# Spreading a triangular solve over the projections' matmuls in the RWKV-7 layer of a two-layer decoder trunk

## Chip, cores and metric

The kernel runs on one core of one Trainium2 chip. The metric is the device time of one execution in microseconds (us); less is better.

## What is computed

The trunk has two layers on a sequence of 512 tokens and a model width of 2048. Each layer is `x + W_out(mixer(RMSNorm(x)) * silu(gate))`. The first layer's mixer is a differential attention, the second's is RWKV-7 time mixing with 32 heads of 64 channels. The change lies in the second layer alone. Its core is a recurrence on a 64x64 state `S` per head:

```python
def step(S, inp):
    r_t, w_t, k_t, v_t, a_t, b_t = inp
    sa = jnp.einsum('bhvk,bhk->bhv', S, a_t)
    S = S * w_t[:, :, None, :] + sa[..., None] * b_t[:, :, None, :] + v_t[..., None] * k_t[:, :, None, :]
    y = jnp.einsum('bhvk,bhk->bhv', S, r_t)
    return S, y
```

Around it, `p = h @ w_in` gives r, k, v and the gate (2048 columns each) and two small low-rank inputs; the token shift mixes each row with the one before; r, k, v and the decay enter the recurrence; the result is normalised per head, gated and projected with `w_out`. All of it is float32.

## The kernel before

**Precision and tiles.** A float32 product is made of three matmuls of split halves (`mm3`, line 129): every weight tile is cast by ScalarE (ACT) into a high half `wh` (line 115), and VectorE (DVE) subtracts it to get the low half `wl` (line 116). One projection of 128 columns takes 16 row blocks of 3 matmuls, so 48 matmuls of 128x512.

**Pairs.** The second layer (`layer1`) works on 16 pairs of heads, `j` = 0 to 15. For each pair it runs four projections on TensorE (PE): v, k of the next pair, the gate of pair `j - 3`, and r of the next pair. All else of the layer is put beside those 192 matmuls.

**Chunked recurrence.** The 512 steps are cut into 8 chunks of 64. For each pair:

- `gram` (line 1099) makes the products of keys and queries inside the chunks into `G`; ACT copies the parts that the solve needs into `LP` (line 1108).
- `t_solve` inverts the unit triangular matrices of all chunks at once, by halves of 32. On DVE it is one transposition into `LT` (line 1158), 31 dependent steps of two instructions each (line 1169 into `tmpl`, line 1171 into `Tm`), a scaling (line 1172) and two transpositions, into `T1` (line 1174; the profile calls the tile T) and `W` (line 1177). GpSimd (POOL) copies `W` into `TT` (line 1182).
- `t_first` (line 1196, PE tile `px`) and `t_second` (line 1211) join the halves; `t_first` reads `T1`, and `t_second` reads `W`.
- `scan_pair` is the recurrence over the chunks. Each chunk goes PE (line 1288), ACT (`rhs`, line 1291), PE (line 1299), ACT (`VS`, line 1301), PE (line 1306), DVE (two state updates into `VS`, one per head, line 1310; line 1313 for the first chunk). The next chunk's line 1288 reads both updates. POOL copies the state aside (`SA`, line 1294) and scales it (`Sg`, line 1297).

While pair `j` is solved, the scan of pair `j - 1` runs. A `Chain` holds the scan as a generator: it is advanced from `tick`, which `mm3` calls after each projection matmul, and each `yield` says how many matmuls are to pass before the next step (7 and 8 for most pairs).

**What sets the order.** The code is traced in Python; a scheduler then puts each engine's instructions in one queue by priority and by its own estimate of when each could start, and every engine works its queue strictly in that order. Priorities are offsets: `AHEAD` 2000 for the weight splits, `SCAN` 3000 for the steps of the scan, `SOLVE` 4000 for the whole of `t_solve`. `issue_after` and `add_manual_dep` with `NoSync` only bind the scheduler's order; no semaphore comes of them.

**Small work of a pair that matters below.** When the chunk's state update has been traced, one piece of `g.later` is traced behind it. The first piece, `decays`, is a DVE scan `l` (line 1049), `m` (1051) and a subtraction into `l` (1052), which ACT turns into `E` (lines 1053 and 1054), `l` (1055) and `BK` (1063). `norms` (lines 1019 and 1020) sums the squares of the keys, split by ACT into `sHx` (line 892) and by DVE into `sLx` (line 893).

Of the kernel before, what the change touches and what calls it, by code (L numbers as in the profile page):

```python
# [23 lines left out]
P = 128  # L24
# [11 lines left out]
    pass  # L36


AHEAD, SCAN, SOLVE = 2000, 3000, 4000


def ahead(offset):


    def deco(f):
        def g_(g, *a, **k):
            with g.tc.high_priority(offset=offset):
                return f(g, *a, **k)

        return g_  # L50

    return deco
# [34 lines left out]
class Halves:  # L87


    def __init__(self, parts, n):  # L90
        self.parts, self.n = parts, n
# [43 lines left out]
class Chain:  # L135
# [7 lines left out]
    def step(self, g):  # L143
        with g.tc.high_priority(offset=SCAN):
            self.wait = next(self.steps, None)
        if g.state and g.later:
            with g.tc.issue_after(g.state.ins):
                g.later.pop(0)()
        g.state = None
        if self.wait is None:  # L150
            g.chains.remove(self)

    def finish(self, g):
        while self.wait is not None:
            with g.tc.issue_after(g.m.ins):
                self.step(g)


def tick(g, m):

    g.m = m
    if g.chains:
        c = g.chains[0]
        c.wait -= 1
        if c.wait <= 0:
            with g.tc.issue_after(m.ins):
                c.step(g)
# [436 lines left out]
def flat(t):  # L604

    n = "abc"[: len(t.shape) - 1]
    n = " ".join(n)
    return t[:].rearrange(f"p {n} -> p ({n})").rearrange("p (k c) -> p k c", k=KG)
# [531 lines left out]
def turn_keys(g, p, c0):  # L1140

    nc = g.nc
    if not c0:
        p.BKT = g.work.tile([P, NC_, P], F32, name="BKT", tag="BKT", bufs=2)
    ps = g.ps.tile([P, 512], F32, name="pt", tag="pb", bufs=2)
    for i in range(4):
        nc.tensor.transpose(ps[:, i * P : (i + 1) * P], p.BK[:, c0 + i].rearrange("p s t -> p (s t)"), g.ident[:])
    nc.scalar.copy(p.BKT[:, c0 : c0 + 4], ps[:].rearrange("p (c k) -> p c k", c=4))


@ahead(SOLVE)
def t_solve(g, j, p):


    nc, w = g.nc, g.work
    NQ = HALF // NG
    LT = w.tile([P, HALF, HALF], F32, name="LT", tag="LT", bufs=1)
    nc.vector.transpose(LT[:].rearrange("p (r c) t -> p t r c", r=NG),  # L1158
                        p.LP[:].rearrange("p c t -> p t c")[:, :, None, :].to_broadcast([P, HALF, NG, NC_]))
    Tm = w.tile([P, NQ, HALF], F32, name="Tm", tag="Tm", bufs=1)  # L1160
    tmp = w.tile([P, NQ * HALF], F32, name="tmpl", tag="tmpl", bufs=1)
    nc.gpsimd.tensor_copy(Tm[:], g.unit[:])
    n2 = p.n2
    nc.vector.tensor_scalar(n2[:], n2[:], 1e-24, None, ALU.max)
    nc.vector.reciprocal(n2[:], n2[:])
    for i in range(HALF - 1):
        n, s = HALF - 1 - i, i // NG + 1
        tt = tmp[:, : n * s].rearrange("p (a b) -> p a b", a=s)
        nc.vector.scalar_tensor_tensor(tt, LT[:, i : i + 1, i + 1 :].to_broadcast([P, s, n]), n2[:, i : i + 1],  # L1169
                                       Tm[:, 0:s, i : i + 1].to_broadcast([P, s, n]), ALU.mult, ALU.mult)  # L1170
        nc.vector.tensor_add(Tm[:, 0:s, i + 1 :], Tm[:, 0:s, i + 1 :], tt)  # L1171
    nc.vector.tensor_mul(Tm[:], Tm[:], n2[:, None, :].to_broadcast([P, NQ, HALF]))
    p.T1 = w.tile([P, NC_, HALF], F32, name="T1", tag="T1", bufs=1)
    nc.vector.transpose(p.T1[:].rearrange("p c (q r) -> p q r c", r=NG),
                        Tm[:].rearrange("p q (r c) -> p q r c", r=NG))
    p.W = w.tile([P, NC_, HALF], F32, name="W", tag="Tm", bufs=1)
    nc.vector.transpose(p.W[:], p.T1[:])
    for h in range(2):
        for half in range(2):
            o = half * HALF  # L1180
            q = slice(h * C + o, h * C + o + HALF)
            nc.gpsimd.tensor_copy(g.TT[j % 2][q, :, h, o : o + HALF], p.W[q])
# [5 lines left out]
def t_first(g, j, p):  # L1188

    nc, w = g.nc, g.work  # L1190
    p.X = w.tile([P, NC_, HALF], F32, name="X", tag="X", bufs=1)
    p.px = px = g.ps.tile([P, 512], F32, name="px", tag="pd", bufs=1)
    N = NC_ * HALF
    for c in range(NC_):
        for h, b0, lo, hi in BLOCKS:
            nc.tensor.matmul(px[hi, c * HALF : (c + 1) * HALF], p.G[lo, c, 0, h, HALF:C], p.T1[lo, c, :],
                             start=True, stop=True, tile_position=(b0, b0 + HALF))
    for _, _, _, hi in BLOCKS:
        nc.scalar.copy(p.X[hi], px[hi, :N].rearrange("p (c s) -> p c s", c=NC_))
    for h, b0, _, _ in BLOCKS:  # L1200
        r_ = slice(b0, b0 + C)
        nc.scalar.copy(p.G[r_, :, 0, h, :], p.AR[r_, :, 0, :])
# [168 lines left out]
def layer1(g, aps):  # L1371
    nc, tc = g.nc, g.tc
    with ExitStack() as cx:
# [7 lines left out]
        def proj(i, j, **k):  # L1381
            return unit_chan(g, [(win, i * D + j * P, P)], P, **k)[0]
# [23 lines left out]
        for j in range(D // P):  # L1406
            p = pairs[j]
            if j:
                others = [(0, lambda p=p: turn_keys(g, p, 0)), (1, lambda p=p: turn_keys(g, p, 4)),
                          (4, lambda p=p: turn_values(g, p))]  # L1410
                if j > 1:
                    others.append((5, lambda i=j - 2: finish_y(g, i, pairs[i])))
                full = LAG <= j < D // P - 1
                gaps = (7, 8) if full else (5, 6) if j < LAG else (4, 5)
                chain(g, j - 1, pairs[j - 1], 3, *gaps, others)
            stage2(g, j, r, p)

            def behind(m, j=j, p=p):
                if j > 1:
                    pairs[j - 2].chain.finish(g)  # L1420
                with tc.issue_after(m.ins):
                    gram(g, j, p)
                mask_gram(g, p, 0)
                mask_gram(g, p, 1)
                t_solve(g, j, p)
                if j > 1:
                    group_norm(g, j - 2, pairs[j - 2])

            stage_v(g, j, p, proj(2, j, behind=[(18, behind)]))
            if j == 0:  # L1430
                turn_keys(g, p, 0)
                turn_keys(g, p, 4)
                turn_values(g, p)
            if j + 1 < D // P:
                begin(j + 1)
            if j >= LAG:
                gated(g, j - LAG, pairs[j - LAG], gate(g, j - LAG, proj(3, j - LAG)))
            if j + 1 < D // P:
                r = receptances(j + 1)
# [29 lines left out]
        def all_sums(n, _):  # L1469
            if n >= 4 * len(sums) + 2 and len(sums) < NS // KG:  # L1470
# [3 lines left out]
                else:  # L1474
                    frow = [w.tile([P, KG, 512], F32, name="frow", tag=t, bufs=1)[:] for t in ("LT", "BK")]
                sums.append(sum_forms(g, g.yd2, len(sums), frow, homes))
# [29 lines left out]
        def banks(i):  # L1506
            if i == 0:
# [3 lines left out]
        Ts = [flat(x) for x in g.TT] + [w.tile([P, KG, 512], F32, name="T2", tag="BK", bufs=1)]  # L1511
        load = loader(g, aps["rw_w_out"][0], ((g.wraw, "wraw", 3), (w, "G1", 2), (g.wraw, "wraw", 3), (w, "LT", 1),
                                              (g.wraw, "wraw", 3), (w, "G1", 2)))
# [3 lines left out]
@with_exitstack  # L1517
def body(ctx, tc, nc, aps):
    g = Ctx()
    g.nc, g.tc = nc, tc  # L1520
    g.last, g.first = None, []
    g.chains, g.later, g.state = [], [], None
    g.const = ctx.enter_context(tc.tile_pool(name="const", bufs=1))
    g.hp = ctx.enter_context(tc.tile_pool(name="hp", bufs=16))
    g.wraw = ctx.enter_context(tc.tile_pool(name="wrawp", bufs=3))
    g.wh = ctx.enter_context(tc.tile_pool(name="whp", bufs=4))
    g.wl = ctx.enter_context(tc.tile_pool(name="wlp", bufs=4))
    g.small = ctx.enter_context(tc.tile_pool(name="small", bufs=3))
    dr = ctx.enter_context(tc.tile_pool(name="dr", bufs=1, space=DRAM))
    g.yd = dr.tile([D, T], F32, name="yd")  # L1530
    g.yd2 = dr.tile([D, T], F32, name="yd2")
    g.xd = aps["x1"] if "x1" in aps else dr.tile([T, D], F32, name="xd")
    g.nd = dr.tile([2, 2, 2, NG, NC_, HALF], F32, name="nd")
    g.ident = g.const.tile([P, P], F32, name="ident")
    make_identity(nc, g.ident)
    for n, layer in ((4, layer0), (2, layer1)):
        with tc.tile_pool(name="pp", bufs=n, space=PSUM) as g.pp, \
                tc.tile_pool(name="ps", bufs=1, space=PSUM) as g.ps:
            layer(g, aps)
# [21 lines left out]
```

## Time and profile before

| | |
|---|---|
| median of 3 runs | 2202.12 us (2201.08 to 2203.34) |
| the profiled execution's own time | 2198.94 us |
| its span, first to last instruction | 2197.2 us |
| granted TensorE clock | 1.000 |
| second layer with all four projections a pair, 12 pairs | about 1190 to 1950 us of the span |
| one such pair, from one `gram` to the next | 63.2 us |

A row of the timeline gives the start in us, the duration in us, the engine, the line, the operation, the tiles (out<-in), the shape and how many instructions are merged; in brackets stands how long the engine had been idle before it and which engine, tile and line ended that wait. A row of the waits gives the total in us, the number of times, and the longest. A row of the costliest groups gives the busy us, the mean ns of one instruction, and the idle time ahead.

### The profile page before, as it was taken

To read this page: it belongs to the slowest core of one execution; us is meant where nothing else is said; L and a number is where in the kernel's file an instruction comes from. 1 tells how busy PE (TensorE), PEld (TensorE's weight loads), DVE (VectorE), ACT (ScalarE), POOL (GpSimd) and SP (SyncE) were. 2 spreads that over 40 slices of the span, in tenths; PEclk is the share of its full clock that TensorE was granted. 3 is DMA by queue.
4 is the path that set the end of the run, shared out by engine and by line. 5 is a ranking of instruction groups with operands and counts; after the bars stand their busy time and mean duration, and the time that the engine had idled before them with its cause. 6 is when DMAs were issued, how large, how long until landed. Compare 5 with 4: busy or idle time off the path is not lost.

```text
span 2197.2 us, 34826 instructions
## 1 busy us (share of the span) xinstructions
PE 2143.5 (98%) x12260; PEld 1751.9 (80%) x12260; DVE 1522.4 (69%) x4137; ACT 1122.5 (51%) x2523; POOL 327.9 (15%) x614
## 2 busy tenths in 40 slices
PE   9999999999999999999899999999999999999999
PEld 7888888888888878878777777777777777777887
DVE  5665646555665667476888788888777888777645
ACT  6444434344443454446566655655566565655323
POOL 0000000000000000120233222222222222232001
PEclk9999999999999999999999999999999999999999
DMA  6323222232223356653222222223222322345556
GB/s 193 98 79 102 80 96 96 87 96 87 96 78 102 129 167 227 155 125 90 70 61 70 75 75 75 61 74 83 69 73 75 83 63 73 83 122 183 173 165 123
DMA packets 258623, 225.76 MB, mean 103 GB/s; under 512 B 12336, under 2 KB 220480, under 8 KB 258448
## 3 DMA queue, kind: packets, MB, share of 16 engines
q1 hardware_dynamic: 239504, 188.03, 28.7%
q0 software_dynamic: 10080, 19.50, 4.5%
q10 hardware_dynamic: 8864, 16.01, 2.0%
q8 instruction: 96, 1.57, 0.3%
q14 instruction: 79, 0.65, 0.1%
HBM read 207.50 MB, written 15.99 MB: 102 GB/s over the span
## 4 chain that ended last, share of the span: by engine, by line
PE 74%; DVE 17%; ACT 5%; issue 3%; DMA 1%; ACTq 0%; DVEq 0%
PE pp L129 57%; PE pt L129 5%; DVE tmpl L1169 4%; DVE Tm L1171 3%; DVE wl L116 3%; DVE VS L1310 2%; ACT G L1103 1%; DVE LT L1158 1%; PE o L129 1%; PE sc L129 1%; PE lora L129 1%; PE gp L1099 1%; PE sm L1288 1%; ACT wh L115 1%; PE Y L1328 1%
## 5 line engine op out<-in xcount | busy, mean ns | idle before, releaser
L116 DVE TENSOR_TENSOR wl<-wraw,wh 128x512 fp32r<-128x512 f32 (+1 forms) x636 | 449.9, 709 | 457.2 <-ACT wh L115 441.2
L115 ACT CAST wh<-wraw 128x512 fp32r<-128x512 f32 (+1 forms) x636 | 393.0, 619 | 530.1 <-PE pp L129 426.9
L129 PE MATMUL pp<-wh,hH 128*128 128x512 f32 x1268 | 500.2, 394 | 1.0 <-DVE prmin_rw_mu_dram L210 0.6
L129 PE MATMUL pp<-wh,hL 128*128 128x512 f32 x1268 | 497.6, 393 | 0.1
L129 PE MATMUL pp<-wl,hH 128*128 128x512 f32 x1268 | 497.2, 392 | 0.0
L129 PE MATMUL pp<-hH,wh 128*128 128x512 f32 x1024 | 416.1, 406 | 0.0
L129 PE MATMUL pp<-hL,wh 128*128 128x512 f32 x1024 | 412.8, 403 | 0.0
L129 PE MATMUL pp<-hH,wl 128*128 128x512 f32 x1024 | 412.5, 403 | 0.0
L129 PEld LDWEIGHTS pp<-wh,hH 128*128 128x128 f32 x1268 | 238.3, 188 | 49.4 <-issue 1.3
L129 PEld LDWEIGHTS pp<-wh,hL 128*128 128x128 f32 x1268 | 238.2, 188 | 49.1 <-DVE hL L884 0.5
L129 PEld LDWEIGHTS pp<-wl,hH 128*128 128x128 f32 x1268 | 238.3, 188 | 46.9
L129 PEld LDWEIGHTS pp<-hH,wh 128*128 128x128 f32 x1024 | 193.0, 188 | 37.3 <-issue 1.4
L129 PEld LDWEIGHTS pp<-hH,wl 128*128 128x128 f32 x1024 | 193.2, 189 | 33.1 <-issue 0.2
L129 PEld LDWEIGHTS pp<-hL,wh 128*128 128x128 f32 x1024 | 193.2, 189 | 31.9
L1294 POOL COPY SA<-VS 64x64 f32<-64x64 f32 x224 | 74.7, 334 | 478.4 <-DVE VS L1310 397.0
L1169 DVE SCALAR_TENSOR_TENSOR tmpl<-LT,n,Tm 128x60 f32<-128x60 f32 (+24 forms) x496 | 135.7, 274 | 14.6
L476 POOL DMA_DIRECT2D frow<-yd x12 | 8.9, 742 | 797.7 <-DVE rs_t L67 675.9
L1171 DVE TENSOR_TENSOR Tm<-Tm,tmpl 128x60 f32<-128x60 f32 (+24 forms) x496 | 104.4, 211 | 12.6
L1291 ACT COPY rhs<-sm 64x64 f32<-64x64 f32 x256 | 52.5, 205 | 84.3 <-PE sm L1288 82.3
L1301 ACT COPY VS<-sm 64x64 f32<-64x64 f32 x256 | 52.8, 206 | 68.4 <-PE sm L1299 63.2
L1288 PEld LDWEIGHTS sm<-VS,G 128*128 128x128 f32 x256 | 43.8, 188 | 50.0 <-PE pp L129 34.8
L1288 PE MATMUL sm<-VS,G 128*128 128x128 f32 x256 | 53.3, 290 | 22.6 <-DVE VS L1310 22.2
(339 smaller groups left out, 3249.5 us busy)
## 6 DMA issues: line engine op xcount, KB each, us to landing
wraw<-in_rw_w_in_dram SPq DMA_DIRECT2D x128, 512.0 KB, 4.0
wraw<-in_da_w_in_dram SPq DMA_DIRECT2D x254, 256.0 KB, 2.9
wraw<-in_da_w_out_dram SPq DMA_DIRECT2D x26, 512.0 KB, 4.3
wraw<-in_rw_w_out_dram SPq DMA_DIRECT2D x26, 512.0 KB, 4.1
yr<-yd SPq DMA_DIRECT2D x28, 256.0 KB, 3.6
frow<-yd POOLq DMA_DIRECT2D x12, 512.0 KB, 6.9
xq<-in_x_dram SPq DMA_DIRECT2D x16, 256.0 KB, 5.1
xd<-xq ACTq DMA_DIRECT2D x16, 256.0 KB, 4.2
```

The lines of the kernel that those rows point to most:

```text
L115: nc.scalar.copy(hi[:], raw[:, k : k + n])
L116: nc.vector.tensor_sub(lo[:], raw[:, k : k + n], hi[:].bitcast(F32))
L129: m = nc.tensor.matmul(out, a, b, start=s, stop=e, skip_group_check=skip)
L1099: m = nc.tensor.matmul(gp[h][:, i * P : (i + 1) * P], BK[r_, c0 + i, :, :], p.AR[r_, c0 + i, :, :], start=True, stop=True)
L1103: nc.scalar.copy(p.G[:, c0 : c0 + 4, :, h, :], gp[h][:].rearrange("p (u x t) -> p u x t", u=4, x=2))
L1169: nc.vector.scalar_tensor_tensor(tt, LT[:, i : i + 1, i + 1 :].to_broadcast([P, s, n]), n2[:, i : i + 1], Tm[:, 0:s, i : i + 1].to_broadca ...
L1171: nc.vector.tensor_add(Tm[:, 0:s, i + 1 :], Tm[:, 0:s, i + 1 :], tt)
L1288: nc.tensor.matmul(sm[:, 0:P], both(p.G[:, c, 0]), both(VS[:, c]), start=True, stop=True)
L1291: nc.scalar.copy(rhs[r_, :], sm[r_, h * C : h * C + C])
L1294: nc.gpsimd.tensor_copy(p.SA[r_, c - 1, :], VS[r_, c, h, :])
L1301: nc.scalar.copy(VS[r_, c, h, :], sm[r_, P : P + C])
L1310: g.state = nc.vector.scalar_tensor_tensor(VS[r_, c + 1, h, :], s_, p.gam[r_, c : c + 1], Sg[r_, :], ALU.mult, ALU.add)
```

## The change

`t_solve` becomes a generator: it yields once at its start (12 matmuls) and after each of the 31 steps (3 or 4 matmuls in turn). A new class `Solve` holds it, and `tick` advances it as the projection matmuls go by, under the same priority. The first instruction of each step gets a `NoSync` dependence on the matmul at which it was traced, so the scheduler does not put it earlier than that matmul by its own clock; the instruction itself waits for no PE semaphore. `t_first` first runs what is left of the solve. `SCAN` goes from 3000 to 5000, so the scan's steps stand above the solve. The number and the kind of the instructions stay as they were on every engine.

```diff
-AHEAD, SCAN, SOLVE = 2000, 3000, 4000
+AHEAD, SCAN, SOLVE = 2000, 5000, 4000
...
+class Solve:
+    def __init__(self, g, steps):
+        self.steps = steps
+        g.solve = self
+        self.step(g)
+
+    def step(self, g, m=None):
+        g.at = m
+        with g.tc.high_priority(offset=SOLVE):
+            self.wait = next(self.steps, None)
+        if self.wait is None:
+            g.solve = None
+
+    def finish(self, g):
+        while self.wait is not None:
+            self.step(g)
...
 def tick(g, m):
     g.m = m
+    if g.solve:
+        g.solve.wait -= 1
+        if g.solve.wait <= 0:
+            g.solve.step(g, m)
...
-@ahead(SOLVE)
+def behind(g, ins):
+    if g.at:
+        g.tc.add_manual_dep(ins.ins, g.at.ins.name, mybir.DependencyInfo(mybir.DependencyClass.NoSync,
+                            mybir.DependencyReason.DATA), reason="pace")
+
 def t_solve(g, j, p):
...
+    yield 12
...
     for i in range(HALF - 1):
...
-        nc.vector.scalar_tensor_tensor(tt, LT[:, i : i + 1, i + 1 :].to_broadcast([P, s, n]), n2[:, i : i + 1],
+        st = nc.vector.scalar_tensor_tensor(tt, LT[:, i : i + 1, i + 1 :].to_broadcast([P, s, n]), n2[:, i : i + 1],
                                        Tm[:, 0:s, i : i + 1].to_broadcast([P, s, n]), ALU.mult, ALU.mult)
+        behind(g, st)
         nc.vector.tensor_add(Tm[:, 0:s, i + 1 :], Tm[:, 0:s, i + 1 :], tt)
+        yield 3 + i % 2
...
 def t_first(g, j, p):
...
+    p.solve.finish(g)
...
-                t_solve(g, j, p)
+                p.solve = Solve(g, t_solve(g, j, p))
```

PE's queue is the same but for the first three pairs, for the place of line 1020 (some matmuls later), and for a few rows near the end of the layer. SP's queue is the same, and so is the whole first layer. What moves is the order on DVE, and with it some of ACT and POOL. The rows below are of the eighth pair, `j` = 7, one of the twelve full pairs. In the changed file the lines stand 24 to 34 further down: 1169 is 1200 there, 1171 is 1203, 1310 is 1344, 1174 is 1207, 1177 is 1210, 1049 is 1073, 1052 is 1076, 1054 is 1078, 1291 is 1325 and 1301 is 1335.

DVE's queue around the third state update of line 1310 (`VS<-sm,gam,Sg`, one row per head) in the scan, before:

```order
L1171 TENSOR_TENSOR Tm<-Tm,tmpl 128x5x14
L1169 TENSOR_SCALAR tmpl<-LT,n_14732,Tm 128x65
L1171 TENSOR_TENSOR Tm<-Tm,tmpl 128x5x13
L1310 TENSOR_SCALAR VS<-sm,gam,Sg 64x64
L1169 TENSOR_SCALAR tmpl<-LT,n_14732,Tm 128x60
L1310 TENSOR_SCALAR VS<-sm,gam,Sg 64x64
L1171 TENSOR_TENSOR Tm<-Tm,tmpl 128x5x12
L116 TENSOR_TENSOR wl<-wraw,wh 128x512
```

The same update in the changed kernel:

```order
L1200 TENSOR_SCALAR tmpl<-LT,n_14732,Tm 128x68
L1203 TENSOR_TENSOR Tm<-Tm,tmpl 128x4x17
L1200 TENSOR_SCALAR tmpl<-LT,n_14732,Tm 128x64
L1203 TENSOR_TENSOR Tm<-Tm,tmpl 128x4x16
L1344 TENSOR_SCALAR VS<-sm,gam,Sg 64x64 x2
L1200 TENSOR_SCALAR tmpl<-LT,n_14732,Tm 128x75
L116 TENSOR_TENSOR wl<-wraw,wh 128x512
```

The two heads' updates now stand side by side, and 16 of the 31 steps stand ahead of them where 19 stood. For the second update it is 9 steps and a half where it was 11, for the fourth 22 where it was 29 and a half, for the fifth 28 where it was all 31.

The end of the solve in DVE's queue, down to the fifth state update, before (`T_14985` is `T1`):

```order
L1171 TENSOR_TENSOR Tm<-Tm,tmpl 128x8
L1051 TENSOR_SCALAR m<-l 128x8
L1172 TENSOR_TENSOR Tm<-Tm,n_14732 128x256
L1052 TENSOR_TENSOR l<-l,m 128x512
L1174 STREAM_TRANSPOSE T_14985<-Tm 128x32x8
L116 TENSOR_TENSOR wl<-wraw,wh 128x512
L1177 STREAM_TRANSPOSE W<-T_14985 128x256
L116 TENSOR_TENSOR wl<-wraw,wh 128x512
L1310 TENSOR_SCALAR VS<-sm,gam,Sg 64x64 x2
```

The same end in the changed kernel (`T_15338` is `T1`), down to the sixth and last update:

```order
L1203 TENSOR_TENSOR Tm<-Tm,tmpl 128x8x2
L1085 TENSOR_TENSOR l<-mixk,l 128x512
L1200 TENSOR_SCALAR tmpl<-LT,n_14732,Tm 128x8
L1203 TENSOR_TENSOR Tm<-Tm,tmpl 128x8
L1205 TENSOR_TENSOR Tm<-Tm,n_14732 128x256
L1207 STREAM_TRANSPOSE T_15338<-Tm 128x32x8
L116 TENSOR_TENSOR wl<-wraw,wh 128x512
L1210 STREAM_TRANSPOSE W<-T_15338 128x256
L1344 TENSOR_SCALAR VS<-sm,gam,Sg 64x64 x2
L949 TENSOR_SCALAR mixv<-pp,prmin_rw_mu_dram,mixv 128x511
```

`T1` moved from ahead of the fifth update to behind it, and five other wide passes over 128x512 (line 1085 is the last of them) now stand ahead of it.

ACT's queue behind the scan step of the chunk in which `decays` runs, before:

```order
L115 COPY wh<-wraw 128x512
L1053 ACTIVATE E<-m 128x8
L1063 ACTIVATE BK<-th_15215,prm_bk_b_1233,prm_bk_s_1230 128x8x64
L1291 COPY rhs<-sm 64x64 x2
L1054 ACTIVATE E<-l 128x8x64
L1055 ACTIVATE l<-l 128x512
L1301 COPY VS<-sm 64x64 x2
L115 COPY wh<-wraw 128x512 x2
```

The same in the changed kernel:

```order
L115 COPY wh<-wraw 128x512
L1077 ACTIVATE E<-m 128x8
L1078 ACTIVATE E<-l 128x8x64
L1325 COPY rhs<-sm 64x64 x2
L1079 ACTIVATE l<-l 128x512
L1087 ACTIVATE BK<-th_15184,prm_bk_b_1233,prm_bk_s_1230 128x8x64
L115 COPY wh<-wraw 128x512
L1335 COPY VS<-sm 64x64 x2
```

`E<-l`, which reads DVE's `l`, now stands ahead of `rhs`, and `BK` and a weight cast `wh` stand ahead of the copy into `VS`.

More of the change, by code (lines that the diff above doesn't have):

```diff
@@ L1521, in body @@
     g.last, g.first = None, []
-    g.chains, g.later, g.state = [], [], None
+    g.chains, g.later, g.state, g.solve = [], [], None, None
     g.const = ctx.enter_context(tc.tile_pool(name="const", bufs=1))
```

## Prediction

> **What bounds the kernel now.** I read the page first: how busy each engine is, and what one step of the solve costs.
>
> ```profile
> PE 2143.5 (98%) x12260; PEld 1751.9 (80%) x12260; DVE 1522.4 (69%) x4137; ACT 1122.5 (51%) x2523; POOL 327.9 (15%) x614
> PE 74%; DVE 17%; ACT 5%; issue 3%; DMA 1%; ACTq 0%; DVEq 0%
> L1169 DVE SCALAR_TENSOR_TENSOR tmpl<-LT,n,Tm 128x60 f32<-128x60 f32 (+24 forms) x496 | 135.7, 274 | 14.6
> L1171 DVE TENSOR_TENSOR Tm<-Tm,tmpl 128x60 f32<-128x60 f32 (+24 forms) x496 | 104.4, 211 | 12.6
> ```
>
> PE is the bound, yet the chain that ended last spends 17% on DVE. A step of the solve is 0.274 + 0.211 us with some 0.03 us before each: 0.54 us, 31 times a pair. Next, what PE waits for:
>
> ```profile
> PE sm L1288 <- DVE VS L1310: 22.2, 40, 1.4
> PE sm L1299 <- ACT rhs L1291: 11.4, 13, 0.9
> PE px L1196 <- DVE T L1174: 3.8, 3, 1.9
> ```
>
> These 56 waits are all that DVE's order can give back in the second layer: 37.4 us as shown. Where they come in a pair, and what they really cost, stands in the stretch from one `gram` to the next, first in the busy times of the engines there, then in PE's timeline:
>
> ```profile
> 1442.83:1506.05 63.22, 60.86 (x421) 49.12 (x420) 50.72 (x140) 37.67 (x91) 17.02 (x35) 1.00 0.27 74
> ```
>
> ```profile
> 1452.74 0.39 PE L129 MATMUL pp<-hH,wh 128*128 128x512 f32 x1
> 1452.97 0.39 PE L129 MATMUL pp<-hL,wh 128*128 128x512 f32 x1
> 1454.13 0.46 PE L1288 MATMUL sm<-VS,G 128*128 128x128 f32 x2 [0.78 <-DVE VS L1310]
> ...
> 1460.97 0.46 PE L1288 MATMUL sm<-VS,G 128*128 128x128 f32 x2 [0.36 <-DVE VS L1310]
> 1467.27 0.46 PE L1288 MATMUL sm<-VS,G 128*128 128x128 f32 x2 [0.29 <-DVE VS L1310]
> 1472.43 0.38 PE L1306 MATMUL sm<-VS,BKT 128*128 128x128 f32 x2
> 1477.99 0.43 PE L1299 MATMUL sm<-rhs,TT 128*128 128x64 f32 x2 [0.93 <-ACT rhs L1291]
> 1479.94 0.38 PE L1306 MATMUL sm<-VS,BKT 128*128 128x128 f32 x2
> 1487.39 0.69 PE L1196 MATMUL px<-T,G 32*32 32x32 f32 x32
> 1494.58 0.40 PE L1019 MATMUL pt<-sHx,ones 128*2 128x512 f32 x1
> 1505.07 0.38 PE L1306 MATMUL sm<-VS,BKT 128*128 128x128 f32 x2
> ```
>
> The first row is the stretch's length, then the busy us of PE, its weight load, DVE, ACT and POOL: DVE has 20% free. A wide matmul's row lasts 0.39 us, but the next starts 0.23 us after it. So a wait costs 0.16 us more than its bracket says: 0.94, 0.52, 0.45 and 1.09 us, 3.0 us of a pair's 63.2. For all 56 waits that is 37.4 + 56 x 0.16 = 46 us, the most that can be won. DVE's rows tell why the updates are late:
>
> ```profile
> 1453.69 0.29 DVE L1310 SCALAR_TENSOR_TENSOR VS<-sm,gam,Sg 64x64 f32<-64x64 f32 x1
> 1474.16 0.27 DVE L1310 SCALAR_TENSOR_TENSOR VS<-sm,gam,Sg 64x64 f32<-64x64 f32 x1
> 1474.55 0.29 DVE L1310 SCALAR_TENSOR_TENSOR VS<-sm,gam,Sg 64x64 f32<-64x64 f32 x1
> 1475.02 1.27 DVE L1049 TENSOR_TENSOR_SCAN l<-rmask,th 128x512 f32<-128x512 bf16 x1
> 1476.80 0.69 DVE L1052 TENSOR_TENSOR l<-l,m 128x512 f32<-128x512 f32 x1
> 1477.41 0.61 DVE L1174 STREAM_TRANSPOSE T<-Tm 128x256 f32<-128x256 f32 x1
> 1483.14 0.75 DVE L1060 SCALAR_TENSOR_TENSOR AR<-mixk,prm_nkk,E 128x512 f32<-128x512 f32 x1
> 1483.81 0.68 DVE L116 TENSOR_TENSOR wl<-wraw,wh 128x512 fp32r<-128x512 f32 x1
> 1505.53 0.59 DVE L1313 TENSOR_SCALAR VS<-sm,gam 64x64 f32<-64x64 f32 x2
> ```
>
> At 1505.07 PE issues line 1306 and the update starts 0.46 us later: that is an idle queue. At 1472.43 the update starts 1.73 us later, and its two halves start 0.39 us apart with half a solve step between them, where a pair put together takes 0.59 us in all. The solve has filled DVE's queue ahead of them.
>
> **The change part by part.** Nothing is added to any engine; by the order, the solve's steps wait for DVE alone. I walk one pair, on the clock of before, and keep the sum of what PE has won. A wide pass moves the queue on by about 0.65 us (1483.14 to 1483.81 is 0.67).
>
> *First update.* It loses the half step between its halves: done at 1453.6 where it was 1453.98. Of 0.94 us, 0.38 go; 0.56 stay, because the transposition `LT` and two steps still stand ahead. Won: 0.38.
>
> *Second.* Behind the first stand 7.5 steps and 3 wide passes: 1453.6 + 4.05 + 1.95 + 0.6 for the pair = 1460.2, and line 1288 follows 0.15 us later (1453.98 to 1454.13 before). PE would be there at 1460.97 - 0.52 - 0.38 = 1460.07: 0.28 stay of 0.52. Won: 0.62.
>
> *Third.* 6.5 steps and 2 wide passes: 1460.2 + 3.5 + 1.3 + 0.6 = 1465.6. PE is there at 1467.27 - 0.45 - 0.62 = 1466.2: nothing stays. Won: 1.07.
>
> *Fourth.* 6 steps and 3 wide passes take the queue to 1470.8; PE's line 1306 stands at 1472.43 - 1.07, and 0.46 later is 1471.8. Here DVE waits for PE, and the pair ends at 1472.4. Behind it comes `decays`, on which ACT hangs:
>
> ```profile
> 1476.59 0.22 ACT L1053 ACTIVATE E<-m 128x8 f32<-128x8 f32 x1 [0.90 <-DVE m L1051]
> 1476.70 0.80 ACT L1063 ACTIVATE BK<-th,prm_bk_b,prm_bk_s 128x512 f32<-128x512 f32 x1
> 1477.52 0.42 ACT L1291 COPY rhs<-sm 64x64 f32<-64x64 f32 x2
> 1477.96 0.63 ACT L1054 ACTIVATE E<-l 128x512 f32<-128x512 f32 x1
> 1478.63 0.63 ACT L1055 ACTIVATE l<-l 128x512 f32<-128x512 f32 x1
> 1479.28 0.44 ACT L1301 COPY VS<-sm 64x64 f32<-64x64 f32 x2
> 1479.74 0.62 ACT L115 CAST wh<-wraw 128x512 fp32r<-128x512 f32 x1
> ```
>
> From the pair's end to the end of line 1052 it was 2.65 us (1474.84 to 1477.49); a half step and the scaling of `Tm` leave that stretch, about 0.45: 1474.6. ACT now runs `E<-l` (0.65) before `rhs` (0.42): 1475.7, and PE wants it at 1477.99 - 1.09 - 1.07 = 1475.83. So the 1.09 goes. Won: 2.16. **But ACT gives part back**: behind `rhs` stand `l` 0.65, `BK` 0.75 and `wh` 0.6 ahead of the copy into `VS` (0.44), which ends at 1478.15; PE wants it at 1479.94 - 2.16 = 1477.78. A new wait of 0.4 us at line 1306. Left: 1.76.
>
> *Fifth update and the end of the solve.* 6 steps, `decays` and 2 `wl` take DVE to about 1478.5, PE's matmul to 1478.6, so the pair ends at 1479.2. Five wide passes, three steps of 0.45 us, the scaling 0.35 and the transposition 0.6 follow: `T1` at 1484.8. PE's `px` stands at 1487.39 - 1.76 = 1485.6. **The cover was 9.4 us (1477.41 + 0.61 to 1487.39) and is now 0.8 us.** I price it at nothing; each us beyond 0.8 costs PE a us a pair.
>
> *Behind `px`.* By the order of ACT, `thg`, two small operations and a DMA's issue now stand ahead of `sHx`, which line 1019 reads:
>
> ```profile
> 1487.33 0.63 ACT L1249 ACTIVATE thg<-mixv 128x512 f32<-128x512 f32 x1 [0.82 <-DVE mixv L925]
> 1492.93 0.61 ACT L892 CAST sHx<-k 128x512 fp32r<-128x512 f32 x1
> ```
>
> `sHx` was done at 1493.54, 1.04 us before line 1019. `thg` is 0.63; with the rest I estimate 1.3, so 0.3 us of new wait at line 1019, between 0 and 1.
>
> A pair wins 1.76 - 0.3 = 1.46 us; twelve full pairs 17.5 us.
>
> *First three pairs.* The three waits for T (3.8 + 3 x 0.16 = 4.3 us) go, since by the order `px` stands 26 to 29 matmuls later there. In the first of them `px`, the copy of `X`, `t_second` and the first scan step now follow one another closely; nothing in the trace shows that, so it is between 0 and 2.5 us, and I take 1.3. Net 3.
>
> *POOL.* The four copies of `W` moved behind the new place of line 1177, next to the sixth update and the passes after it:
>
> ```profile
> 1454.38 0.48 POOL L1297 TENSOR_SCALAR Sg<-SA,gam 128x64 f32<-128x64 f32 x1
> 1475.30 1.23 POOL L1297 TENSOR_SCALAR Sg<-SA,gam 128x64 f32<-128x64 f32 x1
> 1478.94 1.73 POOL L1182 COPY TT<-W 32x256 f32<-32x256 f32 x4 [2.41 <-DVE W L1177]
> ```
>
> The same POOL operation took 0.48 us and 1.23 us beside the scan of line 1049: the two engines do get in each other's way, here at POOL's cost. Before, the copies ran between `W` and the fifth update. `TT` is wanted only by the next pair's line 1299, so I price the move at nothing; at worst DVE stands still for the copies' 1.73 us. The Trainium skill ("SBUF — State Buffer", Who interferes with whom) says that a VectorE instruction with two SBUF inputs and a GpSimd instruction that reads SBUF lock each other out for a whole instruction, and that the order of issue decides who waits. By that rule the 1.73 us could fall on DVE in full, which is the second rival.
>
> **The sum.** 17.5 + 3 = 20.5 us off the profiled execution's 2198.94: 2178.4. That execution was 3.2 us under the median of the runs, 2202.12; on that scale 2181.6, so 2182.
>
> **The rivals.**
>
> *T1 too late (slower).* If the steps behind the fourth update slip by 3 us, because each of them now queues behind passes that wait for ACT's casts, `px` waits 2.2 us a pair: 12 x (2.2 - 1.46) = 9 us lost, less the 3 of the first pairs: 2208. It decides from a slip of 2.5 us on. For it speaks the cover of 0.8 us; against it that all durations in the walk are from rows, and that DVE has 20% of the pair free.
>
> *POOL's copies on DVE's path (no change).* If 1.7 us a pair reach line 1019 through DVE, the 17.5 + 3 become 20.5 - 20.8: 2202. Against it: that stretch had slack, and the sharing seen costs one operation 0.75 us.
>
> *All waits go.* If ACT keeps up and the second update is in time, a pair wins 2.4 us or more: 12 x 2.4 + 4 = 33: 2169.
>
> *No effect.* The dependences bind only the compile-time order, but the queue of DVE does differ, so that this does nothing is not to be expected.
>
> **How the numbers follow.** Forecast 0.60, all waits gone 0.15, POOL's path 0.13, T1 too late 0.12. The forecast's own ends: 0.5 us a pair and 1 us from the first pairs (7 us, 2195), and 2.2 us a pair and 4 (30 us, 2172). The range, 2169 to 2199, takes in the faster rival's point and leaves out the slower one and most of the third. A measurement of this kernel can tell about 0.2%, 4.4 us, from no change. Faster: 0.60 + 0.15 and a third of POOL's case, 0.79; same 0.09; slower 0.12.
>
> **What would show it.** Right: both updates of line 1310 side by side; the waits of line 1288 for them down from 22 us to about 12; those of line 1299 for `rhs` near nothing; new ones of line 1306 for `VS` of about 0.2 us in the profile's count; no wait of `px` for T; 61.7 to 61.9 us from `gram` to `gram`. Wrong: `px` waiting for T in full pairs, line 1019 waiting by more than 1 us, or the pair still at 63.2.

## The result, and the profile after

The changed kernel takes 2183.6 us against 2201.6 us before, a ratio of 0.991 (95% interval 0.989 to 0.993). One of its four runs was disturbed (7472 us) and stands in that median; the other three are 2180.2, 2180.95 and 2186.3 us. The profiled execution is the 2186.3 us one. A second profile of the same kernel, taken later beside two variants (`after_again` below), is of an execution of 2180.9 us.

Rows of the page, then waits of PE, in the first of the two profiles (line 1322 was 1288, 1340 was 1306, 1043 was 1019, 1333 was 1299, 1230 was 1196):

```profile
PE 2147.5 (98%) x12260; PEld 1756.3 (80%) x12260; DVE 1524.7 (70%) x4137; ACT 1120.4 (51%) x2523; POOL 328.0 (15%) x614
PE 79%; ACT 8%; DVE 8%; issue 3%; DMA 1%; ACTq 0%; POOL 0%; DVEq 0%; POOLq 0%
L1200 DVE SCALAR_TENSOR_TENSOR tmpl<-LT,n,Tm 128x60 f32<-128x60 f32 (+24 forms) x496 | 135.2, 272 | 13.2
```

```profile
PE sm L1322 <- DVE VS L1344: 13.9, 16, 2.4
PE sm L1340 <- ACT VS L1335: 3.2, 14, 0.3
PE pt L1043 <- ACT sHx L916: 2.8, 14, 0.2
PE sm L1333 <- ACT rhs L1325: 1.1, 2, 0.8
PE px L1230 <- DVE T L1207: 0.3, 1, 0.3
```

The work is the same; DVE's share of the chain fell from 17% to 8%. Of 37.4 us of waits for DVE's order, 15.3 us are left, and lines 1340 and 1043, which had 0.6 us before, now have 6.0 us. Three pairs by their stretch from one `gram` to the next, then PE's rows of the first of them:

```profile
1375.20:1437.00 61.80, 60.77 (x421) 49.14 (x420) 49.67 (x137) 37.49 (x91) 17.22 (x34) 1.00 0.28 75
1437.00:1501.60 64.60, 62.18 (x421) 50.41 (x420) 53.27 (x141) 37.60 (x91) 17.09 (x34) 0.97 0.26 72
1687.30:1752.20 64.90, 61.98 (x421) 50.30 (x421) 53.77 (x144) 37.55 (x91) 16.96 (x35) 0.97 0.26 72
```

```profile
1386.32 0.46 PE L1322 MATMUL sm<-VS,G 128*128 128x128 f32 x2 [0.56 <-DVE VS L1344]
...
1410.55 0.49 PE L1340 MATMUL sm<-VS,BKT 128*128 128x128 f32 x2 [0.21 <-ACT VS L1335]
1418.10 0.69 PE L1230 MATMUL px<-T,G 32*32 32x32 f32 x32
1425.55 0.40 PE L1043 MATMUL pt<-sHx,ones 128*2 128x512 f32 x1 [0.20 <-ACT sHx L916]
```

Ten of the twelve full pairs look like the first row: 61.5 to 62.0 us where it was 63.2. Three short waits stand where four longer ones stood. DVE's rows of the same pair show why:

```profile
1385.57 0.60 DVE L1344 SCALAR_TENSOR_TENSOR VS<-sm,gam,Sg 64x64 f32<-64x64 f32 x2
1391.97 0.59 DVE L1344 SCALAR_TENSOR_TENSOR VS<-sm,gam,Sg 64x64 f32<-64x64 f32 x2
1397.46 0.60 DVE L1344 SCALAR_TENSOR_TENSOR VS<-sm,gam,Sg 64x64 f32<-64x64 f32 x2
1404.14 0.60 DVE L1344 SCALAR_TENSOR_TENSOR VS<-sm,gam,Sg 64x64 f32<-64x64 f32 x2 [0.79 <-PE sm L1340]
1416.32 0.65 DVE L1207 STREAM_TRANSPOSE T<-Tm 128x256 f32<-128x256 f32 x1
```

The halves of an update stand together, and at the fourth update DVE waits for PE, not PE for DVE. `T1` is ready at 1416.97, 1.1 us ahead of `px`.

**Two pairs are 2.8 and 3.1 us longer than the others**, which nobody had forecast. In the first of them, on DVE, POOL and PE:

```profile
1436.73 0.18 DVE L1195 TENSOR_SCALAR n<-n 128x32 f32<-128x32 f32 x1 [0.97 <-DMA n<-nd]
...
1440.38 0.54 DVE L67 TENSOR_TENSOR rs_t<-rs_i 128x8 f32<-128x8 f32 x1
1441.69 1.61 DVE L1393 TENSOR_TENSOR yc<-yc,rsg 128x512 f32<-128x512 f32 x1
1443.22 1.64 DVE L116 TENSOR_TENSOR wl<-wraw,wh 128x512 fp32r<-128x512 f32 x1
1444.78 2.18 DVE L1189 STREAM_TRANSPOSE LT<-LP 128x1024 f32<-128x1024 f32 x1
```

```profile
1441.61 2.72 POOL L1160 TENSOR_SCALAR_AFFINE_SELECT G<-G 64x1024 f32<-64x1024 f32 x2
```

```profile
1449.45 0.46 PE L1322 MATMUL sm<-VS,G 128*128 128x128 f32 x2 [1.89 <-DVE VS L1344]
```

DVE stood 0.97 us for the DMA into `n`. That pushed the group norm's chain beside POOL's masks, where an `rs_t` of 0.17 us took 0.54 and `yc`, 0.69 us in the pair before, took 1.61. In the pair before, DVE had stood idle for 1.36 us between `yc` and that `wl`, which took 1.53 us beside the masks there too; this slack was used up. The first update came 1.3 us later, and PE waited 1.89 us in place of 0.56. The rest of the 2.8 us is PE's clock, at half for 3.4 us behind that wait (length, PE's busy us, granted clock, DMA share, GB/s):

```profile
1449.00:1451.00 2.00, 1.55 (x7) 0.91 0.03 8
1451.00:1453.00 2.00, 2.00 (x7) 0.50 0.00 0
1453.00:1455.00 2.00, 2.00 (x9) 0.74 0.81 211
```

### The profile page after: what moved, and what is told of

The parts are those of the page before. It is cut to its first block, busy times and chain, and to the rows that moved or that the text cites. A ratio compares the mean times of both kernels' runs of the same rounds, so it can differ in the third digit from the quotient of the medians.

```text
span 2184.6 us, 34849 instructions
## 1 busy us (share of the span) xinstructions
PE 2147.5 (98%) x12260; PEld 1756.3 (80%) x12260; DVE 1524.7 (70%) x4137; ACT 1120.4 (51%) x2523; POOL 328.0 (15%) x614
## 4 chain that ended last, share of the span: by engine, by line
PE 79%; ACT 8%; DVE 8%; issue 3%; DMA 1%; ACTq 0%; POOL 0%; DVEq 0%; POOLq 0%
PE pp L129 61%; PE pt L129 5%; ACT wh L115 1%; DVE wl L116 1%; PE o L129 1%; PE sc L129 1%; DVE LT L1189 1%; PE sm L1340 1%; PE sm L1322 1%; ACT G L1127 1%; PE lora L129 1%; PE gp L1123 1%; DVE VS L1344 1%; PE sm L1333 1%; DVE l L1073 1%
## 5 line engine op out<-in xcount | busy, mean ns | idle before, releaser
L1344 DVE SCALAR_TENSOR_TENSOR VS<-sm,gam,Sg 64x64 f32<-64x64 f32 x192 | 53.8, 280 | 24.9 <-PE sm L1340 20.5
```

Source lines behind the costliest of these rows:

```text
L1344: g.state = nc.vector.scalar_tensor_tensor(VS[r_, c + 1, h, :], s_, p.gam[r_, c : c + 1], Sg[r_, :], ALU.mult, ALU.add)
```

## The experiments

A state update (line 1344 here) is line 1310, 1343, 1345 or 1348 in some of the variants, as edits shift the lines; the other lines move likewise.

**The priority alone.**

```diff
 (the kernel before)
-AHEAD, SCAN, SOLVE = 2000, 3000, 4000
+AHEAD, SCAN, SOLVE = 2000, 5000, 4000
```

> The kernel before with one edit: SCAN goes from 3000 to 5000, the solve is not spread. The queue of VectorE then has each pair of state updates side by side, but about as many solve steps between two pairs of updates as before (8.5, 8, 10 after the first, second and third update, where the changed kernel has 8, 6.5 and 5.5). Theory A (the spreading of the steps brings most of it): by the prediction's own walk a pair wins 0.4 us at the first update, nothing more at the second, and the wait for rhs stays near 1 us, because the chunk's decays still stand behind 10 steps: 0.5 us a pair, 12 pairs 6 us, the first three pairs 1 to 2 us: 2193 to 2195 us. Theory B (the priority alone does it, the spreading is only decoration): 61.8 us a pair and 2180 to 2184 us. Both expect no wait of VectorE for the DMA into n in full pairs, since the norms keep the order of before.

Measured: 2198.7 us, ratio to the kernel before 0.9990 (0.9981 to 0.9999). PE's rows of one pair:

```profile
1390.47 0.46 PE L1288 MATMUL sm<-VS,G 128*128 128x128 f32 x2 [0.53 <-DVE VS L1310]
1397.44 0.46 PE L1288 MATMUL sm<-VS,G 128*128 128x128 f32 x2 [0.50 <-DVE VS L1310]
1403.87 0.46 PE L1288 MATMUL sm<-VS,G 128*128 128x128 f32 x2 [0.41 <-DVE VS L1310]
1414.44 0.43 PE L1299 MATMUL sm<-rhs,TT 128*128 128x64 f32 x2 [0.77 <-ACT rhs L1291]
```

All four waits are there, 2.21 us where they were 2.36, and the pair takes 63.07 us. The first wait is 0.25 us shorter, but the second and the third are 0.14 and 0.12 longer: the half step that stood between the halves of an update now stands ahead of the next one. Theory A holds in kind; it had 0.5 us a pair and 2193 to 2195 us in all, and it was 0.15 us a pair. Two stretches are 64.0 us, both behind a wait of DVE of 1.1 us for the DMA into `n`, which neither theory expected.

**The spreading alone.**

```diff
 (the changed kernel)
-AHEAD, SCAN, SOLVE = 2000, 5000, 4000
+AHEAD, SCAN, SOLVE = 2000, 3000, 4000
```

> The changed kernel with SCAN back at 3000, under the solve's 4000: steps spread, updates not put ahead. Half a step again lies between the two halves of the first and second update. Theory A: the first update waits 0.94 us again in place of 0.55, the second and third wait for nothing since only 6 to 7 steps stand between them, the wait for rhs is gone: 62.2 us a pair against 61.8, so 12 x 0.4 = 5 us more than the changed kernel, 2186 to 2189 us. Theory B (the priority does it): waits of line 1322 back at 0.94, 0.5 and 0.45, 63 us a pair, 2197 to 2202 us.

Measured: 2181.6 us, 0.992 (0.990 to 0.993); one of five runs took 2186.3. The first update is split again on DVE, and its wait is longer:

```profile
1385.51 0.28 DVE L1344 SCALAR_TENSOR_TENSOR VS<-sm,gam,Sg 64x64 f32<-64x64 f32 x1
1385.92 0.29 DVE L1344 SCALAR_TENSOR_TENSOR VS<-sm,gam,Sg 64x64 f32<-64x64 f32 x1
```

```profile
1386.36 0.46 PE L1322 MATMUL sm<-VS,G 128*128 128x128 f32 x2 [0.77 <-DVE VS L1344]
```

0.77 us against 0.56, and 61.95 us a pair against 61.82: the priority is worth 0.13 us a pair, the spreading the other 1.27. That is theory A in kind; it had 62.2 us a pair and 2186 us or more, but against `after_again` PE loses 0.24 us at the first update and wins 0.18 of it back at the second.

**What does the spreading: the order of tracing or the dependence?**

```diff
 (the changed kernel, in t_solve)
-        behind(g, st)
```

> The changed kernel without the ordering dependence: the steps are still traced one by one as the projection matmuls go by, but nothing ties them to those matmuls, and SCAN stays at 5000. Theory O (the dependence does the spreading; the tracing order alone is overridden by the scheduler, which puts a step wherever VectorE is free): on VectorE's queue 8 to 10 steps stand between two state updates as in scan_only, so 63.1 us a pair and 2197 to 2200 us. Rival P (the order of tracing is enough): 61.8 us a pair and 2180 to 2184 us.

Measured: 2198.8 us, 0.9991 (0.9981 to 1.0000), 63.07 us a pair. On DVE 8.5, 8 and 10 steps stand between the first four updates, the same as in scan_only; in the changed kernel it is 7.5, 6.5 and 6. Theory O: without the dependence the scheduler packs the steps again.

**The clamp of n behind the group norm.**

```diff
-    nc.vector.tensor_scalar(n2[:], n2[:], 1e-24, None, ALU.max)
+    behind(g, nc.vector.tensor_scalar(n2[:], n2[:], 1e-24, None, ALU.max))
```

> The changed kernel with the solve's clamp of n bound behind the matmul at which it is traced, as the steps are: on VectorE's queue the clamp and the reciprocal of n move from ahead of the group norm's chain to just ahead of LT, about 5 us later. Theory C (the two pairs of 64.6 and 64.9 us in the changed kernel's profile come from the late DMA into n, which holds VectorE by 1 to 1.5 us and pushes the group norm beside GpSimd's masks): no wait for that DMA in any full pair, all twelve at 61.8 us or a little less (half a step now stands behind the first update, 0.2 us), no granted clock of 0.5 anywhere in them: 2178 to 2181 us in every run. Rival D (the long pairs are a clock dip of TensorE that comes anyhow): pairs of 64.6 us are still there, 2183 to 2186 us.

Measured: 2197.1 us, 0.9980 (0.9971 to 0.9989), both expectations missed by over 10 us. DVE did not wait for the DMA once, no full pair has a granted clock of 0.5 and none is longer than 63.3 us, but the usual pair takes 62.9 us. DVE, then PE:

```profile
1386.39 1.34 DVE L116 TENSOR_TENSOR wl<-wraw,wh 128x512 fp32r<-128x512 f32 x1 [1.55 <-ACT wh L115]
1387.64 1.14 DVE L1195 TENSOR_SCALAR n<-n 128x32 f32<-128x32 f32 x1
1388.82 0.35 DVE L1196 RECIPROCAL n<-n 128x32 f32<-128x32 f32 x1
1389.09 2.08 DVE L1189 STREAM_TRANSPOSE LT<-LP 128x1024 f32<-128x1024 f32 x1
```

```profile
1393.42 0.46 PE L1322 MATMUL sm<-VS,G 128*128 128x128 f32 x2 [1.38 <-DVE VS L1344]
```

The clamp now falls beside the masks and takes 1.14 us where it took 0.18. With the reciprocal behind it, `LT` starts 7.6 us after `gram` where it was 6.4, and the first update's wait goes from 0.55 to 1.40 us. So there is no slack ahead of the first update: what is put there, every pair pays.

**A pause between LT and the first step.**

```diff
 (late_norm)
+    yield 14
     for i in range(HALF - 1):
...
-        yield 3 + i % 2
+        yield 3
```

> late_norm, and between LT and the first step a pause of 14 matmuls, with the steps then 3 matmuls apart (4 after every fourth). On VectorE's queue the first state update stands behind LT and one pass, with no step of the solve ahead of it (before the edit: two steps). Theory E (what is left at the first update is the work of the solve ahead of it): two steps of 0.5 us less ahead of the update, the wait of 0.55 us goes with the 0.16 us behind it, 0.7 us a pair: 61.1 us a pair, 8.5 us under late_norm, 2170 to 2173 us; T1 and px keep their distance of 1.1 us, so no wait there. Rival F (the time goes to the next wait: the later updates, line 1340 for VS, or px, which now has the steps closer together ahead of it): 61.6 to 61.8 us a pair, 2178 to 2181 us.

The kernel as it ran has all steps 3 matmuls apart, without the 4 after every fourth.

Measured: 2179.7 us, 0.990 (0.989 to 0.992), 61.64 us a pair. The two steps are gone from ahead of the update, but the clamp still stands there:

```profile
1386.47 0.46 PE L1323 MATMUL sm<-VS,G 128*128 128x128 f32 x2 [0.45 <-DVE VS L1345]
```

Against late_norm the wait falls by 0.93 us, as theory E has it: from the end of `LT` to the update it is 0.56 us on DVE where it was 1.50. The number that it gave, 61.1, left out what late_norm's clamp had cost. The pair and the total fall into rival F's range, but no other wait of the usual full pair has grown, so its reason does not hold.

**Clamp and steps behind the first update.**

```diff
 (the changed kernel)
-    nc.vector.tensor_scalar(n2[:], n2[:], 1e-24, None, ALU.max)
+    yield 10
+    behind(g, nc.vector.tensor_scalar(n2[:], n2[:], 1e-24, None, ALU.max))
...
-        yield 3 + i % 2
+        yield 3 + (i % 4 == 3)
```

> The changed kernel, with a pause of 10 matmuls between LT and the first step, and the clamp and the reciprocal of n traced behind that pause and bound there (late_norm and gap14n had them just ahead of LT, where the clamp took 1.14 us beside GpSimd's masks); the steps then 3 matmuls apart (4 after every fourth). On VectorE's queue LT and one pass stand ahead of the first state update, no step and no clamp. Theory E (the remaining wait at the first update is the length of what stands ahead of it): LT starts 6.4 us after gram as in the changed kernel, the update starts 2.66 us after LT as in gap14n, so it ends 9.7 us after gram, 0.9 us ahead of PE: no wait of line 1322 in full pairs, 61.0 us a pair (gap14n's 61.64 less 0.45 and 0.16), no wait for the DMA into n; 2171 to 2175 us. Rival F (what is won there is lost at the next wait: the second update, line 1340, or px): 61.4 to 61.6 us a pair, 2177 to 2180 us.

Measured: 2177.6 us, 0.990 (0.988 to 0.991). DVE, then the fourth stretch and the fifth:

```profile
1384.50 2.22 DVE L1189 STREAM_TRANSPOSE LT<-LP 128x1024 f32<-128x1024 f32 x1
1386.57 0.70 DVE L116 TENSOR_TENSOR wl<-wraw,wh 128x512 fp32r<-128x512 f32 x1
1387.30 0.60 DVE L1345 SCALAR_TENSOR_TENSOR VS<-sm,gam,Sg 64x64 f32<-64x64 f32 x2
```

```profile
1191.90:1256.50 64.60, 61.99 (x426) 49.76 (x425) 54.08 (x144) 40.03 (x99) 17.13 (x36) 1.00 0.26 72
1256.50:1317.40 60.90, 60.34 (x422) 49.28 (x421) 50.58 (x141) 37.41 (x91) 16.64 (x34) 1.00 0.27 77
```

Theory E, from the fifth stretch on: PE does not wait at the first update, there is no wait for the DMA into `n`, and the pair takes 60.93 us. The first four stretches take 216.7 us where the changed kernel has 211.0: the solve is late for the short pairs, where PE waits up to 3.2 us for an update, and 1.7 of the 5.7 us is PE's clock, at half for 3.4 us. So the total misses theory E's range, though the profiled run, 2174.4 us, lies in it; the other three took 2177 to 2178 us at a mean clock of 0.996 to 0.997 where it had 0.998.

**POOL's copies doubled.**

```diff
 (the changed kernel, in t_solve)
-            nc.gpsimd.tensor_copy(g.TT[j % 2][q, :, h, o : o + HALF], p.W[q])
+            for _ in range(2):
+                nc.gpsimd.tensor_copy(g.TT[j % 2][q, :, h, o : o + HALF], p.W[q])
```

> The changed kernel with GpSimd's four copies of W into TT of each pair issued twice (eight copies, 1.7 us to 2.6 us more on GpSimd a pair), at the place to which the change moved them. The forecast priced that move at nothing. Theory G (nobody waits for the copies, and VectorE beside them loses under 0.3 us): 61.8 to 61.9 us a pair, 2180 to 2186 us. Rival H (the prediction's second rival: what GpSimd copies, VectorE stands still, and px, line 1043 or the outputs wait for that): at least 1 us a pair, 12 us or more: 2192 to 2205 us.

Measured: 2191.3 us, 0.996 (0.995 to 0.997). The fourth stretch and a full pair further on, then POOL's rows ahead of the fourth stretch:

```profile
1194.50:1261.90 67.40, 63.41 (x421) 51.39 (x420) 54.21 (x145) 37.63 (x91) 19.39 (x39) 0.95 0.25 69
1385.70:1447.50 61.80, 60.71 (x421) 49.12 (x420) 50.86 (x140) 37.46 (x91) 19.70 (x39) 1.00 0.27 75
```

```profile
1186.24 5.32 POOL L1216 COPY TT<-W 32x256 f32<-32x256 f32 x8 [1.32 <-DVE W L1210]
...
1192.31 0.57 POOL L1151 DMA_DIRECT2D n<-nd  x1
```

The total speaks for H, the full pairs but the first for G: most take 61.85 to 61.9 us, 0.05 us more than without. DVE does lose time beside the eight copies: `BK` (line 1091) takes 1.43 us for 1.22, a pass into `mixv` (line 1285) 0.88 for 0.68 and `sLup` (line 917) 0.51 for 0.42. Of this only 0.09 us shows on PE, at line 1043. Of the loss of 10.6 us, 10.5 lie in the first four stretches (221.6 us against 211.1): there PE waits for `TT` itself at line 1334, three times, up to 1.1 us, DVE waits up to 2.95 us for the DMA into `n`, which POOL issues behind the copies, and PE's clock is at half for 10.2 us in all, which is 5.1 us. The price of nothing is right for all full pairs but the first, and the cover is thin ahead of it.

**A slower pace.**

```diff
 (the changed kernel)
-        yield 3 + i % 2
+        yield 4
```

> The changed kernel with every step 4 matmuls after the last one (3 and 4 in turn before): the last step is traced 15.5 matmuls later, about 4.5 us. It stands for the prediction's first rival, in which T1 comes after PE wants it (the cover measured in the changed kernel is 1.1 us). The scheduler by its own estimate puts px 17 matmuls later in PE's queue (152 in place of 135 after gram) and leaves the second join where it was (159). Theory I (a late T1 costs PE what goes beyond the cover): px waits up to 3 us a pair or, where the place of px has moved with it, the second join waits for the copy of X, 1 to 2 us a pair: 2195 to 2215 us. Rival J (the place of px moves with T1, and the 7 matmuls between the joins cover the copy): no new wait over 0.3 us, fewer steps ahead of each update: 61.5 to 62 us a pair, 2178 to 2186 us.

Measured: 2190.8 us, 0.996 (0.994 to 0.997).

```profile
PE px L1230 <- DVE gam L1095: 5.3, 12, 0.5
```

`gam` is the instruction behind `T1` on DVE and ends 0.01 us after it. In full pairs `px` waits 0.45 us, line 1322 waits 0.5 us for the fifth update, and the pair takes 62.25 us in six cases and 61.8 in four: between I and J. After `gram`, `T1` ends 6.1 us later than in the changed kernel, but `px` had been put 17 matmuls later with it. The other 9 us are lost in the first four stretches (220.3 against 211.1); 6.8 of them are PE's clock, which is at half there for 13.7 us.

**The changed kernel again, and the pause kept from the first three pairs.**

> The changed kernel once more, unchanged, beside the two that follow. Theory C (long pairs come where VectorE waits about 1 us or more for the DMA into n, so their number differs from one execution to the next): 2180 us plus 2.9 us for each long pair, so single times between 2180 and 2187 us, and in the profile every long pair behind a wait of VectorE for that DMA of over 0.9 us and every shorter wait without effect. Rival D (TensorE's clock dips by itself): long pairs also where VectorE did not wait for the DMA.

Measured: 2180.7 us (2180.4 to 2183.2), ratio to the kernel before 0.991 (0.989 to 0.992). No long pair; DVE's one wait for the DMA into `n` ahead of a full pair is 0.46 us. Over the profiles of this study, every full pair behind such a wait of 0.97 us or more (five) was longer by 0.8 to 5.5 us, and none behind one of 0.63 or less (five) by more than 0.2. In best_a30 below, where DVE reads `n` later and does not wait, landings of 3.4 and 3.7 us left their pairs at 60.76 and 60.73 us. Theory C stands as far as that goes; the DMA alone was never delayed on purpose, and it is not the only cause: the fourth stretches of gap10a and slow_pace, 64.6 and 66.9 us, had no wait for it.

```diff
 (gap10a)
-    yield 10
+    if j >= LAG:
+        yield 10
...
-        yield 3 + (i % 4 == 3)
+        yield 3 + (i % 4 == 3) if j >= LAG else 3 + i % 2
```

> gap10a for the pairs from the fourth on, the changed kernel's own pace and its early clamp in the first three pairs. Theory K (gap10a's loss lies in the first three pairs and the one behind them, whose solve the pause made late: its first four stretches from gram to gram are 216.7 us, the changed kernel's 211.0): the first three stretches as in the changed kernel, 149.4 us, the fourth 61.0 to 61.5, the others 60.93 as in gap10a: 2168 to 2171 us. Rival L (the long fourth stretch belongs to the pause itself, as the first pair that has it): 2172 to 2176 us.

Measured: 2168.4 us, 0.985 (0.983 to 0.986), the clamp bound only from the fourth pair on. The first three stretches, and the fourth:

```profile
1040.70:1190.20 149.50, 141.67 (x1014) 112.19 (x1013) 124.33 (x349) 95.00 (x224) 42.77 (x83) 1.00 0.25 67
1190.20:1251.20 61.00, 60.44 (x422) 49.28 (x421) 51.21 (x142) 37.48 (x91) 16.91 (x34) 1.00 0.29 80
```

Theory K: the changed kernel's first three stretches, gap10a's full pairs.

```diff
 (best_a, in receptances)
-            behind = [(24, lambda m: norms(g, j, pairs[j], m))]
+            behind = [(30 if j > LAG else 24, lambda m: norms(g, j, pairs[j], m))]
```

> best_a, and the norms of the keys in the full pairs hung 6 matmuls later (30 in place of 24): in PE's queue line 1043 stands three matmuls later, next to line 1044, which itself is one matmul later. Theory M (the new wait of line 1043 for sHx costs its 0.20 us and the 0.16 us behind it, as the others do): 0.36 us a pair less, 60.6 us a pair, about 4 us under best_a. Rival N (so short a wait is hidden behind the matmul before it, or comes back at line 1044): 60.9 us a pair and no difference to best_a.

Measured: 2166.0 us, 0.984 (0.982 to 0.985), **the fastest version**: 14.7 us under the changed kernel on the same chip. The wait of line 1043 is gone and the pair takes 60.75 us:

```profile
1371.00:1431.70 60.70, 60.35 (x421) 49.23 (x421) 50.96 (x140) 37.53 (x91) 16.90 (x34) 1.00 0.28 77
```

Between M and N: 0.18 us a pair, the bracket without the 0.16 us behind it.

## Why the prediction was right

The forecast of 2182 us is 1.6 us off the measured median, and 1.3 us from the median of `after_again`. The mechanism is the one forecast: the same work in another order on DVE, with the waits moved as the walk has them. That the number came so close is partly luck, since the terms of a pair miss by up to 0.3 us and the misses cancel. The forecast counts each wait with the 0.16 us behind it; its terms are therefore compared with the distance between PE's starts, in the same full pairs of the profile before and of the two profiles after, the long pairs left out.

- **First update:** 0.38 us to be won; 0.22 to 0.27. The bracket left is 0.53 to 0.56 us in most pairs, with the 0.16 us some 0.7, where the forecast left 0.56 in all. The reason given, the half step between the halves, is borne out: scan_only wins 0.27 there, and pace_only loses 0.24. Over a whole pair the priority is worth only 0.13 to 0.15, since the half step then stands ahead of the second update.
- **Second and third:** 0.24 and 0.45 us to be won; 0.41 to 0.45 and 0.53, and 0.15 more at line 1322 behind the fourth, which the walk left out. From the end of the first update to the end of the second it is 6.4 us, where the walk had 6.6.
- **rhs:** 1.09 us to be won; 0.82. A gap of 0.07 to 0.12 us stays in the full pairs, shorter than the profile lists as a wait.
- **Line 1340 for `VS`:** 0.4 us to be lost, 0.2 in the profile's count; 0.49, and 0.21 to 0.23 in brackets.
- **Line 1043 for `sHx`:** 0.3 us to be lost; 0.30, though best_a30 won back only 0.18 of it.
- **Cover of `px`:** 0.8 us; 1.1. No wait.
- **A pair:** 1.46 us won; 1.4 (63.22 to 61.82). Between the fourth and the last `gram`, 759.6 us became 742.0 in `after_again`: 17.6 us, forecast 17.5. The waits of line 1322 sum to 13.9 us, and to 10.8 in `after_again`, forecast about 12.
- **First three pairs, the mis-sized term:** net 3; measured 0.8 (150.3 to 149.5). The 4.3 us went, but 1.3 us for what comes was too low, as some 3.5 us came: the brackets of lines 1333, 1043 and 1230 sum to 2.0 us in the first profile, six of them, with up to 0.16 us behind each. The rest, about 1 us, stays open.
- **The sum:** 20.5 us off 2198.94; 18.0 in `after_again` (to 2180.92). It is the 17.6 and the 0.8; 1.1 us are lost ahead of the first `gram` and 0.6 won behind the last. Where that `gram` starts differs between the profiles by as much, from 1039.25 to 1040.71 us, so the 1.1 us is not put down to the change.
- **Not in the prediction:** the DMA into `n`. Ahead of the full pairs it landed in 1.8 to 2.3 us in the profile before, and in up to 3.8 us in the first profile after; there 5.9 us of the gain are lost by two pairs. Why it landed later is not shown: the clamp that reads it starts 0.8 us later than before, so in undisturbed pairs it had more slack. scan_only, with the clamp at its old place, has landings of 3.2 us too.

The rivals: "T1 too late" did not come. slow_pace does not test its price: there the scheduler put `px` later along with `T1`, while the rival's slip would come at run time, with PE's queue fixed. "POOL's copies on DVE's path" did not come in full pairs: beside the four copies DVE loses 0.2 us a pair (`gam`, 0.36 us where it took 0.15), not 1.73, and it has slack there. In the first pairs double_copy shows the copies on the path of `TT` and of the DMA into `n`, which is not the way that the rival had. "All waits go" came near with three more edits (2166.0 us in best_a30), and even there line 1340 waits 0.22 us a pair.

## What to carry to other kernels

Where an idle-looking engine feeds a recurrence, what counts is not its share of busy time but how much other work stands in its queue between two steps of the recurrence; here spreading that work with ordering dependences paid ten times as much a full pair as a higher priority did, and tracing it spread without the dependence paid nothing. Look first at what stands ahead of the one step that still waits, and move exactly that; check the short first iterations apart, since gap10a's pace, which suits the steady ones, made the first four stretches nearly 6 us longer. When a change makes the steady part tight, waits for small DMAs and work beside another engine's long instruction can decide which iterations run long, as in the two long pairs here.

## What the hardware showed

**A small DMA's landing scatters, and the order may hide it or not.** The 16 KB of `n` landed in this time, from issue, between 1200 and 1900 us, in the kernel before and in the changed kernel:

```profile
DMA to landing us min/median/max: 1.8/1.9/2.2
DMA to landing us min/median/max: 1.9/2.2/3.8
```

**DVE beside POOL's masks.** `yc` took 1.61 us there for 0.69, a pass `wl` 1.64 for 0.69, the clamp of `n` 1.14 for 0.18 (late_norm). `LT`, with one SBUF input, hardly grew: 2.23 us with its first 1.1 us beside the masks, 2.18 and 2.08 behind them. The Trainium skill ("SBUF — State Buffer", Who interferes with whom) says that a VectorE instruction with two SBUF inputs locks against a GpSimd instruction that reads SBUF, for a whole instruction. The rows of `yc` and `wl` agree with it. The clamp reads one SBUF tile, and by the same section of the Trainium skill could only contend in a 2-port mode; no run here shows which mode it ran in.

**PE's clock after a stall.** The granted clock fell to 0.50 for 3.4 us, in two cases for 6.8 us, and half of that time is lost. It did so at PE's waits of 1.89 and 2.37 us (both long pairs), and also at 2.82 us in slow_pace, 2.94 us in late_norm and 3.41 us in double_copy. It stayed at 1.00 behind 2.25 us in the kernel before and behind 3.20 us in gap10a. Shorter waits did it too: at one of 1.70 to 1.74 us near 981 us, which every profile has, it fell in eleven of the thirteen, and around the short first pairs it fell at waits of 0.8 to 1.2 us (in no_bind, gap14n, gap10a, double_copy and slow_pace). So a wait of 0.9 us can cost 1.7 us and more on top, and its length alone does not decide. The Trainium skill ("TensorE: Matmul & The Clock Gate", Part 1) has the clock halved after an idle window of about 3.4 us that runs freely. The half clock and the part that chance plays agree with it; that waits so much shorter sufficed does not follow from that length.
